# Feed-forward block of a two-layer trunk in fp32 by split products: down product 1 placed between products 3 and 7, gate multiplication later, roundings issued together

## The chip, the cores and the metric

The kernel runs on one core of a Trainium2 chip. Its five engines work side by side: TensorE (PE in the profile) multiplies, VectorE (DVE), ScalarE (ACT) and GpSimd (POOL) work element by element, SyncE (SP) issues transfers; POOL issues some of them too. Each engine takes its instructions in the order in which they were written and waits at the first one whose inputs are not there. The metric is the device time of one execution in microseconds (us), the median of several runs.

## The reference

One sequence of 512 positions, 1024 wide, runs through two layers. Layer 0 mixes with a gated linear recurrence, layer 1 with a stick-breaking attention; behind each mixer stands a feed-forward block of width 2816, and this is what the change is about:

```python
def _swiglu(h, w_gate, w_up, w_down):
    g = h @ w_gate.astype(h.dtype)
    u = h @ w_up.astype(h.dtype)
    return (jax.nn.silu(g) * u) @ w_down.astype(h.dtype)
...
        h = _rmsnorm(x, norm_ffn_g[layer])
        x = x + _swiglu(h, ffn_w_gate[layer], ffn_w_up[layer], ffn_w_down[layer])
```

All inputs and the output are float32.

## The kernel before

**Numbers in two parts.** Every operand of a matrix product is split into a rounded part (high) and what is left (low), and a product is three matmuls: high by high, high by low, low by high. For a weight tile of 128 x 1024 ACT writes the rounded part `wh` (a CAST, line 303), and DVE, or POOL for some tiles, the residual `wl` (a subtraction, line 304). In the profile's names `wh`, `wl` are these; `raw`, `bu`, `bv`, `d`, `dt` are the loaded weights that they come from.

**Seven products for eight.** The two projections up and the projection down are each done by a scheme of the Strassen kind: seven products of half-size blocks take the place of eight, at the price of sums of weights and of results. The products up are called g1 to g7, those down d1 to d7. Sums of weights are partly made by accumulating transfers, issued by POOL (line 92), partly on POOL (`minus`, line 144) and DVE (`sums`, line 164 down, line 116 up). The weights of g3 and g7 lie in `bv`: when g3's tile has been split, a transfer adds onto `bv` what g7 needs.

**Units.** A block of feed-forward goes in six units, u = 0 to 5: units 0 to 4 ("full") take 512 columns each of gate and up, unit 5 (`NU`, the "half unit") 256. From unit 1 on, a unit also does the products down for the columns of the unit before. A full product is two pieces for g (12 matmuls each) and one piece of 12 matmuls for d. `Unit.order` is a list written by hand that sets the program's order; PE, ACT, DVE and POOL keep it exactly. Weights run ahead of the products through one list of pieces: when a piece is used (`chunk`), pieces up to four further are split (`split_one`: ACT's cast and the residual), and up to eleven further are loaded. Split weights have four pairs of buffers, so that a cast also waits until PE is through with the piece four before.

**From one unit to the next.** The step `tt` turns the four results of the unit before, u2 and b5, with PE's transposes into PSUM banks 76, 77 (tb) and 74, 75 (db). `operands1` and `operands2` then make the left operands of the products down from them, first for tb (in `tt`), then for db (steps `o1` and `o2`): copy t, rounded parts `hah`, `hbh`, `hth` on ACT, four reads of the banks into t and the low parts `hal`, `hbl`, `htl` on DVE. d1 reads ha, d2 and d4 hb, the others ht. Where ACT and DVE read the same bank, the later one in the program waits for the earlier one.

**Around the results.** After g6 ACT copies bank A into `u` (line 871), after g3 DVE adds bank B onto it (`u2_add`). After g7 DVE adds bank A onto `b` (b5); g4 goes on accumulating in bank A, so it waits for that addition. After g2 come an addition of r1 and Silu (line 857), after g4 another Silu (line 889). `q1` (line 861) multiplies u2 by the gate of g2, `q2` (line 913) b5 by that of g4. Each down product ends with two additions onto `y` (`dproduct`, line 754); its bank is used again by a later one: d1, d6, d7, d4 share one pair of banks, d2, d5, d3 the other (in the half unit the pairs change places). In the table `mids` stands which of q1, q2 is called between the matmuls of a down product and its additions. Lines 753 and 754 are the helpers for subtractions and additions, 758 the cast of a split, 762 to 764 the three matmuls of a product.

Of the kernel before, what the change touches and what calls it, by code (L numbers as in the profile page):

```python
# [10 lines left out]
F32 = mybir.dt.float32  # L11
# [21 lines left out]
NU = 5  # L33
# [11 lines left out]
class Unit:  # L45
    def __init__(self, kern, l, u):
        self.kern, self.u = kern, u
        self.w = FB if u < NU else FB // 2
        self.np = 2 if u < NU else 1
        self.kt = 2 if u < NU else 4  # L50
        self.src = kern.a["w_gu"][l, 8 * u:8 * u + 4 * self.np]
        self.down = kern.a["w_dn"][l, 4 * (u - 1):4 * u] if u else None
        self.b, self.d = {}, {}
        self.direct = u == NU
        if u == 0:
            self.order = "g1 g5 stats g2 x0 g6 x1 g3 q1 g4 x2 g7 x3"
        elif u < NU:
            self.order = "g5 g1 tt g6 o1 o2 g3 g7 d1 d2 g4 d6 d5 g2 d7 d3 d4"
        else:
            self.order = "g5 g1 tt g6 o1 g3 o2 d1 g2 d2 g7 d6 d5 g4 q2 d7 tn d3 d4"  # L60
        if u == NU - 1:
            self.order = self.order.replace("g2 d7", "g2 q1 d7")
        if u == 1:
            self.order = self.order.replace("g5 g1", "g1 g5")
        self.pieces = []
        for n in self.order.split():
            if n[0] not in "gd":
                continue
            q = int(n[1])
            self.pieces += [Piece(self, q, c) for c in range(self.np)] if n[0] == "g" else [DownPiece(self, q)]  # L70


class Piece:
    LOADS = {1: ("raw", 0), 2: ("raw", 2), 5: ("bu", 0), 3: ("bv", 3)}
    HOME = {1: 1, 2: 2, 5: 5, 6: 5, 4: 5, 3: 3, 7: 3}
    def __init__(self, unit, q, c):
        self.unit, self.q, self.c = unit, q, c
        self.pool = (q, c) == (7, 1) and unit.u > 0 and unit.np == 2
        self.summed = False

    def buf(self, tag, pool, bufs):
# [16 lines left out]
    def load(self):  # L98
        un, kern, q = self.unit, self.unit.kern, self.q
        if q not in self.LOADS:  # L100
            return
        tag, n = self.LOADS[q]
        t = un.b[q, self.c] = kern.raw_buf() if tag == "raw" else self.buf(tag, kern.wp, 2)
        kern.nc.sync.dma_start(t, self.part(n))
        if q == 5:
            self.plus(1)
            kern.chain[self.c] = un
# [25 lines left out]
class DownPiece(Piece):  # L133
# [12 lines left out]
    def load(self):  # L146
        un, kern = self.unit, self.unit.kern
        for k in {1: ("12", "22", "11"), 2: ("21",)}.get(self.q, ()):
            t = un.d[k] = kern.raw_buf() if k in ("11", "21") else self.buf("d" + k, kern.fp, 1)
            kern.nc.sync.dma_start(t, un.down[("11", "21", "12", "22").index(k)])  # L150
        if self.q == 1:
            un.d["t"] = self.buf("dt", kern.fp, 1)
            n = 6 if un.direct else 1
            self.minus("t", "22", "12", n)
            self.minus("12", "12", "11", n + 1)

# [14 lines left out]
class Kern:  # L171
# [554 lines left out]
    def ffn(self, l, gnext):  # L726
        nc, tc = self.nc, self.tc
        mm = nc.tensor.matmul
        E = mybir.EngineType
        with tc.tile_pool(name=f"ffn{l}", bufs=1) as self.fp, \  # L730
# [4 lines left out]
            for i in range(self.used + 1, len(self.chunks)):  # L735
                if isinstance(self.chunks[i], Piece) and not isinstance(self.chunks[i - 1], Piece):
# [3 lines left out]
            db, tb = self.bank[4:6], self.bank[6:]  # L740
            fp = self.fp
            ev = [[fp.tile([P, S], F32, tag=f"{n}{j}", bufs=1, name=f"{n}{j}") for j in range(2)]
                  for n in ("r1", "u2", "b5")]
            r1, u2, b5 = ev
            y = [fp.tile([P, D], F32, tag=f"y{t}", bufs=1, name=f"y{t}") for t in range(NT)]
            ha, hb, ht = ([fp.tile([P, *shape], F32R, tag=f"{n}{i}", bufs=1, name=f"{n}{i}") for i in "hl"]
                          for n, shape in (("ha", (2, HS)), ("hb", (2, S)), ("ht", (2, 4, HS))))
# [5 lines left out]
            sub = lambda o, a, b: nc.vector.tensor_tensor(o, a, b, ALU.subtract)  # L753
            add = lambda o, a, b: nc.vector.tensor_tensor(o, a, b, ALU.add)  # L754

            def split(dst, src):
                h, lw = dst
                nc.scalar.copy(h, src)  # L758
                sub(lw, src, h.bitcast(F32))
# [6 lines left out]
            def turn(fs, banks):  # L766
                for f, b in zip(fs, banks):
                    for t in range(NT):
                        nc.tensor.transpose(b[:, ts(t)], (u2 + b5)[t][:, ts(f)], self.ident)  # L769

            def operands1(p, banks):
                cx = self.tmp()
                nc.scalar.copy(cx, banks[0])
                split([t[:, p] for t in ha], cx[:, T0])
                return cx

            def operands2(p, banks, cx):
                bx, by = banks
                ta, tc_ = (self.tmp() for _ in range(2))
                add(ta[:, T0], cx[:, T1], by[:, T1])  # L780
                sub(tc_[:, T0], cx[:, T0], bx[:, T1])
                sub(ta[:, T1], ta[:, T0], cx[:, T0])
                sub(tc_[:, T1], by[:, T0], ta[:, T1])
                split([t[:, p] for t in hb], by)
                for i, t in enumerate((ta, tc_)):
                    split([o[:, p, 2 * i:2 * i + 2].rearrange("p a b -> p (a b)") for o in ht], t)

# [36 lines left out]
            for u in range(NU + 1):  # L824
                un = self.unit_of()
# [6 lines left out]
                def product(q, out, first=True):  # L832
                    for c in range(un.np):
                        wh, wl = self.chunk()
                        for j in range(2):
                            for i in range(un.kt):
                                k = c * un.kt + i
                                oh, ol = self.ops[k][q]
                                ws = slice(i * w, i * w + w)
                                mm3(out[j][:, :w], oh[:, ts(j)], ol[:, ts(j)], wh[:, ws], wl[:, ws],  # L840
                                    first and k == 0, k == 3)

                def b5_copy():
                    for j in range(2):
                        nc.scalar.copy(b5[j][:, :w], B[j][:, :w])
# [6 lines left out]
                def g2():  # L852
                    product(2, B2)
                    for j in range(2):
                        add(B2[j][:, :w], r1[j][:, :w], B2[j][:, :w])
                    for j in range(2):
                        nc.scalar.activation(B2[j][:, :w], B2[j][:, :w], AF.Silu, scale=rs(j))

                def q1():
                    for j in range(2):  # L860
                        nc.vector.scalar_tensor_tensor(u2[j][:, :w], u2[j][:, :w], nrs(j), B2[j][:, :w],  # L861
                                                       ALU.mult, ALU.mult)
# [59 lines left out]
                def tt():  # L922
                    turn((0, 2), tb)
                    turn((1, 3), db)
                    cx = operands1(0, tb)
                    b5_copy()
                    operands2(0, tb, cx)

                def o1():
                    self.cx = operands1(1, db)  # L930
# [7 lines left out]
                        split([t[:, p] for t in hn], A[p])  # L938

                steps = dict(q1=q1, q2=q2, g1=g1, g2=g2, g3=g3, g4=g4, g5=g5, g6=g6, g7=g7, stats=stats, tt=tt, o1=o1, o2=o2, tn=tn)  # L940
                mids = {6: q2, 7: q1} if u < NU - 1 else {6: q2} if u < NU else {2: q1}
                steps.update({f"d{q}": (lambda q=q: dproduct(q, two, mids.get(q))) for q in range(1, 8)})
                steps.update({f"x{t}": (lambda t=t: None if gnext else turned(t)) for t in range(NT)})
                for n in un.order.split():
# [440 lines left out]
```

## Time and profile before

| what | value |
|---|---|
| median of 3 runs | 1170.92 us (1170.79 to 1173.19) |
| profiled execution, its own time | 1172.12 us |
| its span, first to last instruction | 1170.4 us |
| mean granted clock of TensorE | 0.982 |
| PE, DVE, ACT, POOL busy | 1114.0, 911.0, 711.3, 400.0 us |
| feed-forward blocks in the span | about 167 to 530 and 806 to 1166 us |

Rows of a timeline read: start, duration (us), engine, line, operation, what it writes and from what (buffer numbers left out), shapes, how many in a row, and in brackets how long the engine stood idle before it and what ended that. Full units 1 to 4 of layer 0 have their g7 at 230, 297, 360 and 425 us; the prediction works in unit 3, at 336 to 402 us. In PE's rows the moving operand tells the product: `s` is g7's left operand, `ow` that of g2 to g6, `a` of g1, `hah` d1, `hbh` d2 or d4, `hth` the other down products.

### The profile page before, as it was taken

How to read it: one execution, taken by the hardware profiler on the slowest of the kernel's cores; microseconds unless marked ns; L12 is line 12 of the kernel's file. 1: busy time of each engine (PE TensorE's matmuls, PEld its weight loads, DVE VectorE, ACT ScalarE, POOL GpSimd, SP SyncE). 2: the span in 40 equal slices, each digit the busy share in tenths (PEclk: the TensorE clock that was granted, in tenths of full speed). 3: DMA queues.
4: the chain of work that ended last, by engine and by line, in shares of the span. 5: the costliest groups of instructions: out<-in, count | busy, mean ns of one | idle time of the engine just before them, and what ended most of it. 6: DMA issues, size and time to landing. Idle time of an engine off the chain costs nothing. (4 is left out here: it accounts for less than half of the span.)

```text
span 1170.4 us, 14792 instructions
## 1 busy us (share of the span) xinstructions
PE 1114.0 (95%) x5265; PEld 916.6 (78%) x5265; DVE 911.0 (78%) x1242; ACT 711.3 (61%) x1086; POOL 400.0 (34%) x266
## 2 busy tenths in 40 slices
PE   8999999989998989999999999899989999998987
PEld 6887788778787868878888888778878878787875
DVE  7878886667887868887378898778657797777887
ACT  6698576455545454535479999868654445545454
POOL 2451332344442514115043443412234344342411
PEclk9999999989999989999999999899999999999999
DMA  8422349857575655342243333125966757574421
GB/s 281 153 90 90 109 124 221 177 160 165 129 205 137 182 134 166 91 144 85 76 127 101 100 91 94 52 90 168 217 120 196 158 164 165 137 194 100 143 57 72
DMA packets 48825, 159.87 MB, mean 137 GB/s; under 512 B 6000, under 2 KB 7280, under 8 KB 48752
## 3 DMA queue, kind: packets, MB, share of 16 engines
q1 hardware_dynamic: 36368, 113.84, 28.3%
q0 software_dynamic: 12384, 45.09, 22.1%
q8 instruction: 41, 0.67, 0.2%
q14 instruction: 32, 0.26, 0.1%
HBM read 148.43 MB, written 2.10 MB: 129 GB/s over the span
## 5 line engine op out<-in xcount | busy, mean ns | idle before, releaser
L304 DVE TENSOR_TENSOR wl<-raw,wh 128x1024 fp32r<-128x1024 f32 (+1 forms) x118 | 197.7, 1679 | 59.6 <-ACT wh L303 59.1
L303 ACT CAST wh<-raw 128x1024 fp32r<-128x1024 f32 (+1 forms) x144 | 144.4, 1011 | 96.9 <-PE bank L764 34.6
L762 PE MATMUL bank<-wh,ow 128*128 128x512 f32 (+1 forms) x480 | 179.9, 375 | 2.4 <-DVE u L754 1.8
L764 PE MATMUL bank<-wh,ow 128*128 128x512 f32 (+1 forms) x480 | 178.4, 372 | 0.0
L763 PE MATMUL bank<-wl,ow 128*128 128x512 f32 (+1 forms) x480 | 178.3, 371 | 0.0
L92 POOL DMA_DIRECT2D bu<-w_gu x64 | 56.2, 878 | 223.1 <-DVE wl L304 114.0
L303 ACT CAST wh<-bu 128x1024 fp32r<-128x1024 f32 x66 | 69.4, 1051 | 78.7 <-issue 33.4
L304 DVE TENSOR_TENSOR wl<-bu,wh 128x1024 fp32r<-128x1024 f32 x66 | 82.0, 1249 | 32.2 <-ACT wh L303 31.2
L762 PEld LDWEIGHTS bank<-wh,ow 128*128 128x128 f32 x480 | 90.4, 188 | 19.3 <-DVE u L754 2.6
L349 PE MATMUL bank<-uh,wh 128*128 128x512 f32 x256 | 102.3, 400 | 2.1 <-ACT wh L303 1.4
L764 PEld LDWEIGHTS bank<-wh,ow 128*128 128x128 f32 x480 | 90.4, 188 | 15.7
L763 PEld LDWEIGHTS bank<-wl,ow 128*128 128x128 f32 x480 | 90.5, 188 | 15.4
L351 PE MATMUL bank<-uh,wl 128*128 128x512 f32 x256 | 100.2, 392 | 1.4 <-DVE wl L304 1.4
L350 PE MATMUL bank<-ul,wh 128*128 128x512 f32 x256 | 99.7, 390 | 0.3 <-DVE ul L406 0.3
L304 POOL TENSOR_TENSOR wl<-raw,wh 128x1024 fp32r<-128x1024 f32 (+1 forms) x26 | 59.2, 2278 | 111.9 <-ACT wh L303 111.9
L754 DVE TENSOR_TENSOR y<-y,bank 128x512 f32<-128x512 f32 x140 | 88.9, 678 | 2.4 <-PE bank L764 2.3
L762 PE MATMUL bank<-wh,hth 128*128 128x512 f32 x192 | 75.2, 392 | 4.1 <-DVE y L754 4.1
L763 PE MATMUL bank<-wl,hth 128*128 128x512 f32 x192 | 75.0, 391 | 0.4 <-DVE wl L304 0.4
L764 PE MATMUL bank<-wh,htl 128*128 128x512 f32 x192 | 74.8, 390 | 0.0
L304 DVE TENSOR_TENSOR wl<-bv,wh 128x1024 fp32r<-128x1024 f32 x36 | 49.2, 1366 | 30.8 <-ACT wh L303 29.8
L303 ACT CAST wh<-bv 128x1024 fp32r<-128x1024 f32 x44 | 46.2, 1051 | 40.2 <-DMA bv<-w_gu 29.3
L1135 POOL TENSOR_TENSOR spl<-t,sph 128x512 fp32r<-128x512 f32 (+1 forms) x32 | 36.4, 1159 | 85.7 <-DVE sph L1134 79.8
(258 smaller groups left out, 2844.2 us busy)
## 6 DMA issues: line engine op xcount, KB each, us to landing
bu<-w_gu POOLq DMA_DIRECT2D x64, 512.0 KB, 5.8
raw<-w_gu SPq DMA_DIRECT2D x44, 512.0 KB, 3.5
raw<-w_dn SPq DMA_DIRECT2D x24, 512.0 KB, 5.9
bu<-w_gu SPq DMA_DIRECT2D x22, 512.0 KB, 3.4
bv<-w_gu SPq DMA_DIRECT2D x22, 512.0 KB, 3.5
bv<-w_gu POOLq DMA_DIRECT2D x22, 512.0 KB, 6.3
d<-w_dn SPq DMA_DIRECT2D x20, 512.0 KB, 3.5
raw<-w_qk SPq DMA_DIRECT2D x16, 512.0 KB, 3.4
```

What stands on the lines that cost most here:

```text
L92: kern.soon(lambda: kern.nc.gpsimd.dma_start(t, self.part(n), accum_op=ALU.add))
L303: self.nc.scalar.copy(wh[:, c], raw[:, c])
L304: self.wl_engine(i).tensor_tensor(wl[:, c], raw[:, c], wh[:, c].bitcast(F32), ALU.subtract)
L349: mm(out, lhsT=wh, rhs=xh, start=first, stop=False)
L350: mm(out, lhsT=wh, rhs=xl, start=False, stop=False)
L351: mm(out, lhsT=wl, rhs=xh, start=False, stop=last)
L754: add = lambda o, a, b: nc.vector.tensor_tensor(o, a, b, ALU.add)
L762: mm(out, lhsT=xh, rhs=wh, start=first, stop=False, skip_group_check=True)
L763: mm(out, lhsT=xh, rhs=wl, start=False, stop=False, skip_group_check=True)
L764: mm(out, lhsT=xl, rhs=wh, start=False, stop=last, skip_group_check=True)
L1135: nc.gpsimd.tensor_tensor(sl[:, w], sp[:, w], sh[:, w].bitcast(F32), ALU.subtract)
```

## The change

The diff, complete but for context:

```diff
-            self.order = "g5 g1 tt g6 o1 o2 g3 g7 d1 d2 g4 d6 d5 g2 d7 d3 d4"
+            self.order = "g5 g1 tt g6 o1 o2 g3 d1 g7 d2 g4 d6 d5 g2 d7 d3 d4"
...
-        self.pool = (q, c) == (7, 1) and unit.u > 0 and unit.np == 2
+        self.pool = False
...
-            n = 6 if un.direct else 1
+            n = 6 if un.direct else 3
             self.minus("t", "22", "12", n)
             self.minus("12", "12", "11", n + 1)
...
-            def operands2(p, banks, cx):
+            def operands2(p, banks, cx, mid=None):
                 bx, by = banks
                 ta, tc_ = (self.tmp() for _ in range(2))
+                nc.scalar.copy(hb[0][:, p], by)
+                if mid:
+                    mid()
                 add(ta[:, T0], cx[:, T1], by[:, T1])
                 sub(tc_[:, T0], cx[:, T0], bx[:, T1])
                 sub(ta[:, T1], ta[:, T0], cx[:, T0])
                 sub(tc_[:, T1], by[:, T0], ta[:, T1])
-                split([t[:, p] for t in hb], by)
+                sub(hb[1][:, p], by, hb[0][:, p].bitcast(F32))
...
                     for j in range(2):
                         add(B2[j][:, :w], r1[j][:, :w], B2[j][:, :w])
+                    if u < NU:
+                        silu1()
+
+                def silu1():
                     for j in range(2):
                         nc.scalar.activation(B2[j][:, :w], B2[j][:, :w], AF.Silu, scale=rs(j))

                 def q1():
+                    if u == NU:
+                        silu1()
...
-                    b5_copy()
-                    operands2(0, tb, cx)
+                    operands2(0, tb, cx, b5_copy)
...
-                mids = {6: q2, 7: q1} if u < NU - 1 else {6: q2} if u < NU else {2: q1}
+                mids = {6: q2, 3: q1} if u < NU - 1 else {6: q2} if u < NU else {2: q1}
```

In the full units d1 stands between g3 and g7 instead of behind g7. The second piece of g7 gets its residual on DVE; `pool` of the down pieces is set elsewhere and stays. `hbh` is issued directly behind `hah`, ahead of DVE's four bank reads, and in `tt` ahead of the copies into b5 as well. In units 1 to 3 `q1` moves from d7 to d3; in the half unit Silu of g2 moves into `q1`, behind the splitting that d2 triggers. POOL's two differences of down weights are due two pieces later.

ACT in unit 3 of layer 0, from the cast of g3's second piece on; `bv` are g7's weights, `raw_2709` or `raw_2669` d1's, `raw_2730` d2's. Before:

```order
L303 CAST wh_2833<-bv_2643 128x1024
L303 CAST wh_2850<-bv_2625 128x1024
L871 COPY u_1495<-bank_72 128x512
L871 COPY u_1496<-bank_73 128x512
L773 COPY t_2870<-bank_74 128x512
L758 CAST hah<-t_2870 128x256
L758 CAST hbh<-bank_75 128x512
L758 CAST hth<-t_2874 128x512
L758 CAST hth<-t_2875 128x512
L303 CAST wh_2886<-bv_2643 128x1024
L303 CAST wh_2904<-raw_2709 128x1024
L303 CAST wh_2922<-raw_2730 128x1024
```

The same stretch of ACT now:

```order
L303 CAST wh_2833<-bv_2643 128x1024
L303 CAST wh_2850<-raw_2669 128x1024
L880 COPY u_1495<-bank_72 128x512
L880 COPY u_1496<-bank_73 128x512
L773 COPY t_2870<-bank_74 128x512
L758 CAST hah<-t_2870 128x256
L780 CAST hbh<-bank_75 128x512
L758 CAST hth<-t_2874 128x512
L758 CAST hth<-t_2875 128x512
L303 CAST wh_2886<-bv_2625 128x1024
L303 CAST wh_2904<-bv_2643 128x1024
L303 CAST wh_2922<-raw_2730 128x1024
```

The cast of g7's first piece went from second place to behind the roundings, and d1's cast took its place.

DVE in the same unit, from behind the low parts `htl` on; u are the additions of g3, b those of g7, y those of a down product, and L164 is the sum for d6. Before:

```order
L304 TENSOR_TENSOR wl_2905<-raw_2709,wh_2904 128x1024
L754 TENSOR_TENSOR u_1495<-u_1495,bank_70 128x512
L754 TENSOR_TENSOR u_1496<-u_1496,bank_71 128x512
L304 TENSOR_TENSOR wl_2923<-raw_2730,wh_2922 128x1024
L304 TENSOR_TENSOR wl_2939<-bu_2505,wh_2938 128x1024
L754 TENSOR_TENSOR b_1497<-b_1497,bank_72 128x512
L754 TENSOR_TENSOR b_1498<-b_1498,bank_73 128x512
L304 TENSOR_TENSOR wl_2957<-bu_2527,wh_2956 128x1024
L164 TENSOR_TENSOR raw_2709<-dt_2711,raw_2709 128x1024
L754 TENSOR_TENSOR y_1499<-y_1499,bank_74 128x512
L754 TENSOR_TENSOR y_1500<-y_1500,bank_75 128x512
```

The same stretch of DVE now:

```order
L304 TENSOR_TENSOR wl_2887<-bv_2625,wh_2886 128x1024
L304 TENSOR_TENSOR wl_2905<-bv_2643,wh_2904 128x1024
L754 TENSOR_TENSOR u_1495<-u_1495,bank_70 128x512
L754 TENSOR_TENSOR u_1496<-u_1496,bank_71 128x512
L304 TENSOR_TENSOR wl_2923<-raw_2730,wh_2922 128x1024
L754 TENSOR_TENSOR y_1499<-y_1499,bank_74 128x512
L754 TENSOR_TENSOR y_1500<-y_1500,bank_75 128x512
L304 TENSOR_TENSOR wl_2941<-bu_2505,wh_2940 128x1024
L304 TENSOR_TENSOR wl_2957<-bu_2527,wh_2956 128x1024
L164 TENSOR_TENSOR raw_2669<-dt_2671,raw_2669 128x1024
L754 TENSOR_TENSOR b_1497<-b_1497,bank_72 128x512
L754 TENSOR_TENSOR b_1498<-b_1498,bank_73 128x512
```

The residual of g7's second piece (from `wh_2904`) is new here, and the two additions onto b stand two weight residuals, the sum and two additions onto y further back.

ACT in the half unit of layer 0, from the cast of g7 on; `raw_3498` is d6's sum, `d_265` is d5's weights, `bu_3415` g4's, and the two ACTIVATE rows are Silu of g2. Before:

```order
L303 CAST wh_3806<-bv_3474 128x1024
L303 CAST wh_3827<-raw_3498 128x1024
L857 ACTIVATE bank_70<-bank_70,rsT 128x256
L857 ACTIVATE bank_71<-bank_71,rsT 128x256
L303 CAST wh_3861<-d_265_3494 128x1024
L303 CAST wh_3884<-bu_3415 128x1024
```

The same stretch of ACT in the half unit now:

```order
L303 CAST wh_3806<-bv_3474 128x1024
L303 CAST wh_3827<-raw_3498 128x1024
L303 CAST wh_3859<-d_265_3494 128x1024
L864 ACTIVATE bank_70<-bank_70,rsT 128x256
L864 ACTIVATE bank_71<-bank_71,rsT 128x256
L303 CAST wh_3884<-bu_3415 128x1024
```

Silu went behind the cast for d5.

In units 1 to 3, DVE's two rows of `q1` moved from ahead of the additions of d7 to behind them and behind one more weight residual. POOL's row loses the residual of g7 in every full unit and is otherwise unchanged in order; so is SP's.

## The prediction

> **What bounds the kernel now.** I read the busy shares first, then TensorE's waits, then its granted clock in the stretches that the waits point to, and last the timelines of ACT and DVE there. The busy shares:
>
> ```profile
> PE 1114.0 (95%) x5265; PEld 916.6 (78%) x5265; DVE 911.0 (78%) x1242; ACT 711.3 (61%) x1086; POOL 400.0 (34%) x266
> ```
>
> TensorE (PE) sets the end, so the question is only where it stands still or runs slowly. PE's waits, in total, times and longest:
>
> ```profile
> PE bank L763 <- POOL wl L304: 15.4, 8, 1.9
> PE bank L762 <- ACT wh L303: 10.7, 8, 2.3
> PE bank L762 <- DVE y L754: 5.8, 8, 2.1
> ```
>
> The first two come eight times each: the seventh product of the eight full units (units 1 to 4 of both layers). The table of stretches cuts out that product, from its first matmul to the first one of the next product; the row behind it is a product of the same 24 matmuls, the third product of unit 3, which did not wait. The columns are the stretch and its length, the busy times, the granted clock, and the DMA share:
>
> ```profile
> 230.10:243.26 13.16, 8.69 (x25) 6.13 (x26) 10.77 (x15) 6.74 (x10) 2.36 (x1) 0.74 0.35 105
> 297.30:305.40 8.10, 6.01 (x25) 4.42 (x24) 6.41 (x8) 5.41 (x7) 2.35 (x1) 1.00 0.32 120
> ...
> 1062.63:1073.57 10.94, 7.43 (x25) 5.51 (x24) 9.22 (x13) 5.41 (x7) 2.35 (x1) 0.84 0.15 49
> sum 85.81, PE 59.42 PEld 43.57 DVE 70.48 ACT 45.44 POOL 18.82; mean PE 7.43 PEld 5.45 DVE 8.81 ACT 5.68 POOL 2.35
> 354.50:359.94 5.44, 5.44 (x26) 4.50 (x24) 1.84 (x3) 2.91 (x5) 0.88 (x1) 1.00 0.59 103
> ```
>
> 24 matmuls take 5.44 us when nothing holds them, 0.227 each. Eight times that is 43.5, and the eight took 85.81: **42.3 us are lost in product 7**. The waits make up only 15.4 + 10.7 = 26.1. The rest is in PE's own timeline (start, length, idle before and releaser), unit 3, between the product's two pieces:
>
> ```profile
> 364.15 0.50 PE L762 MATMUL bank<-wh,s 128*128 128x512 f32 x1 [1.33 <-ACT wh L303]
> 366.58 0.80 PE L763 MATMUL bank<-wl,s 128*128 128x512 f32 x1 [1.93 <-POOL wl L304]
> 367.18 0.63 PE L764 MATMUL bank<-wh,s 128*128 128x512 f32 x1
> 367.60 0.63 PE L762 MATMUL bank<-wh,s 128*128 128x512 f32 x1
> ...
> 369.61 0.39 PE L764 MATMUL bank<-wh,s 128*128 128x512 f32 x1
> ```
>
> A matmul's length of 0.39 overlaps the next one's start, so a wait costs its length plus 0.16 (0.39 - 0.227); and behind the two waits the matmuls start 0.42 apart (367.18, 367.60) until the pace is back at 369.61. The granted clock says the same: 0.74 and 0.84 where both waits are long, 1.00 where they add to 2.1 (297.30). The Trainium skill (TensorE: Matmul & The Clock Gate, "What's actually happening") halves the clock after an idle window of about 3.4 us. No single wait here is that long, so by that rule taken wait by wait, product 7 would give back 26.1 + 16 x 0.16 = 28.7 us; the stretches measure 42.3, and I take the measurement.
>
> Why PE waits: ACT and DVE in unit 3.
>
> ```profile
> 356.63 1.05 ACT L303 CAST wh<-bv 128x1024 fp32r<-128x1024 f32 x1 [3.10 <-DMA bv<-w_gu]
> 357.59 1.07 ACT L871 COPY u<-bank 128x512 f32<-128x512 f32 x2
> 361.53 0.59 ACT L758 CAST hbh<-bank 128x512 fp32r<-128x512 f32 x1 [1.95 <-DVE t L753]
> 362.01 1.14 ACT L758 CAST hth<-t 128x512 fp32r<-128x512 f32 x2
> 363.05 1.04 ACT L303 CAST wh<-bv 128x1024 fp32r<-128x1024 f32 x1
> ```
> ```profile
> 361.07 0.43 DVE L753 TENSOR_TENSOR t<-bank,t 128x256 f32<-128x256 f32 x1
> 362.15 0.69 DVE L753 TENSOR_TENSOR hbl<-bank,hbh 128x512 fp32r<-128x512 f32 x1 [0.65 <-ACT hbh L758]
> 362.76 1.28 DVE L753 TENSOR_TENSOR htl<-t,hth 128x512 fp32r<-128x512 f32 x2
> 365.08 2.53 DVE L304 TENSOR_TENSOR wl<-raw,wh 128x1024 fp32r<-128x1024 f32 x1 [1.03 <-ACT wh L303]
> 368.73 1.21 DVE L304 TENSOR_TENSOR wl<-raw,wh 128x1024 fp32r<-128x1024 f32 x1
> 369.86 1.21 DVE L304 TENSOR_TENSOR wl<-bu,wh 128x1024 fp32r<-128x1024 f32 x1
> ```
> ```profile
> 355.14 0.88 POOL L92 DMA_DIRECT2D bv<-w_gu  x1 [6.82 <-DVE wl L304]
> 364.18 2.35 POOL L304 TENSOR_TENSOR wl<-bv,wh 128x1024 fp32r<-128x1024 f32 x1 [8.16 <-ACT wh L303]
> ```
>
> ACT first waits 3.10 for the accumulating load of the first piece of product 7, with the copies of product 6 (u) queued behind it. Then hbh waits 1.95 until DVE has read the same bank four times (last 361.07), DVE's hbl waits 0.65 for hbh, and the cast of the second piece (363.05) stands behind all of it. Its residual on POOL then takes 2.35, while DVE's own residual beside it takes 2.53 against 1.21 to 1.23 elsewhere.
>
> **The change, part by part,** in unit 3; a weight cast costs 1.04 (363.05), a weight residual 1.13 from start to start (368.73, 369.86), a pair of 512-wide adds 1.2 (1.28 for y below, less the overlap), the roundings and bank reads what their rows say.
>
> *Down product 1 between products 3 and 7, roundings together.* ACT now casts down piece 1, loaded long before, at 352.8 where it waited for the load, and copies u when product 6 is through (354.50 in the table, its last bank 354.7), not at 357.59. The first bank-half's chain, changed the same way, hands over about 0.5 earlier. Then t 355.2, hah 355.8, hbh at once 356.1 to 356.7. DVE: hal 356.3, its four bank reads from 356.8 (they now wait for hbh) to 358.3, hbl to 358.9, htl to 360.1. ACT meanwhile hth to 359.0 and the first piece of product 7 to 360.0; DVE's residual of it 360.1 to 361.3. The second piece's load is issued once product 3's second residual is done, so about 354.6 instead of 355.14; with this median (min/median/max, issue to landing)
>
> ```profile
> DMA to landing us min/median/max: 3.4/5.5/10.0
> ```
>
> it is there at 360.1; cast to 361.2, residual, now on DVE, to 362.5. PE, dense: down product 1 at 359.94, product 7 at 362.7, its second piece at 365.4, down product 2 at 368.1, product 4 at 370.8. Down product 1 overwrites the banks that hbl reads last: free at 358.9, margin 1.0. Product 7 has its residuals at 361.3 and 362.5: margins 1.4 and 2.9. Both old waits go. What is late next is DVE, now without a break: u adds to 363.6, residual of down 2 to 364.8, y adds to 366.0, the two residuals of product 4 to 368.3, the sum for down 6 (as wide as a residual) to 369.4, then the b5 additions to 370.6. Product 4 accumulates into the banks they read, bank by bank: first free at 370.0, margin 0.8. Before, two down products covered these additions; now one does. Unit 1 begins late (its loads come later): I allow 0.3 there in each layer. So 42.3 - 0.6 = **41.7 us**. This covers the moved residuals too: 8 x 1.21 more for DVE, of which 2.53 - 1.21 comes back in each unit, because nothing on POOL reads beside it; on the path it costs nothing while the margins of 1.4 and 0.8 hold, else what exceeds them.
>
> POOL's two differences of down pieces keep their place in POOL's row (only their due number changes), SP's row is unchanged, and POOL's next loads no longer stand behind a 2.35 residual: nothing. Down product 7 behind product 4 instead of 1 and 2 before it: no, products 5, 6, 2 and the rest keep their places, nothing.
>
> *Later gate multiplication (L861), units 1 to 3.* Down product 4 adds onto the banks of down product 7 and waits for DVE's y:
>
> ```profile
> 398.17 0.47 PE L762 MATMUL bank<-wh,hbh 128*128 128x512 f32 x1 [0.27 <-DVE y L754]
> 396.03 1.40 DVE L861 SCALAR_TENSOR_TENSOR u<-u,nrs,bank 128x512 f32<-128x512 f32 x2
> 397.34 1.28 DVE L754 TENSOR_TENSOR y<-y,bank 128x512 f32<-128x512 f32 x2
> ```
>
> With the multiplication behind it, y starts at 396.03 and the first bank is free at 396.7, before 397.74 when PE wants it. Six of the eight y waits are these, 0.27 to 0.28 each: 6 x (0.27 + 0.16) = **2.6 us**. The multiplication then stands before the y adds of down product 3; the banks that it reads are next written by product 1 of the next unit, three products later: nothing.
>
> *The half unit (unit 5).* Same order; the roundings and the place of Silu change.
>
> ```profile
> 485.24 0.39 PE L762 MATMUL bank<-wh,ow 128*128 128x256 f32 x1 [0.89 <-DVE u L754]
> 499.32 0.47 PE L762 MATMUL bank<-wh,hth 128*128 128x512 f32 x1 [2.09 <-DVE y L754]
> 478.60 0.59 ACT L758 CAST hbh<-bank 128x512 fp32r<-128x512 f32 x1 [3.39 <-DVE t L753]
> 494.76 0.81 ACT L857 ACTIVATE bank<-bank,rsT 128x256 f32<-128x256 f32 x2 [1.63 <-DVE bank L754]
> 498.50 1.28 DVE L754 TENSOR_TENSOR y<-y,bank 128x512 f32<-128x512 f32 x2
> ```
>
> hbh waits 3.39 for DVE's bank reads; issued at once, the chain hands over 1.0 earlier (0.65 of DVE's wait, and hth no longer stands behind 0.59 of hbh). So down 1 no longer waits for hah, and product 2 starts at 484.25 instead of 485.24. The second chain gives another 0.9. Dense from there, down product 5 would start at 495.4. It needs the y adds, which stood behind the residual of down 5, whose cast stood behind Silu (494.76). With Silu behind that cast, the residual ends at 494.3, the multiplication at 495.1, the first y at 495.7: start 495.8 instead of 499.32, 3.5 us earlier; both layers, **7.0 us**. Lower bound: if the chains give nothing, the order of Silu alone gives about 1.5 each, 3.0.
>
> *Sum.* 41.7 + 2.6 + 7.0 = 51.3. I keep 1.3 back for margins below 1 us that fail in some unit. The profiled execution took 1172.12 (span 1170.4), so 1122.1; the median of the runs shown is 1.2 below it: **1121 us**. Own range of this case: 1115 (no loss left, and small waits such as that for L913 gone too) to 1127 (margins missed by 0.7 in every unit).
>
> **Rivals.**
> 1. *The wait moves to down product 1 or to product 4.* For it: margins of 1.0 and 0.8 after a chain of some twenty steps. Against: every step has its own row. If DVE or ACT is 1.8 us late per unit, PE waits 0.8 to 1.0 more and 0.16, eight times, 8 to 9 us; 3 us late, 18 us: 1130 to 1139.
> 2. *The load of product 7's second piece.* At the slowest landing, 10.0, it is there at 364.6 and its residual at 366.9: PE waits 1.5, and the b5 additions behind it on DVE are late by about as much: 3 x 8 = 24, so 1145 if all units meet it. The median landing and the margin of 2.9 speak against it.
> 3. *DVE becomes the bound.* From down 1 to down 1, unit 2 to unit 3:
>
> ```profile
> 305.40:370.53 65.13, 61.32 (x270) 49.75 (x269) 53.38 (x60) 32.23 (x41) 26.42 (x15) 0.97 0.64 162
> ```
>
> DVE is busy 53.38 of 65.13; shortened by 5 it would be at 89%. If its idle stretches could shrink by only half of 5.3, units would lose 2.6 and not 5.3: half of 41.7 is left out, 1142. Against it: the idle that goes (the 1.03 and 0.65 above among it) lies just where the change works. The Trainium skill (Perfetto Trace Analysis, "Optimizing Scalar/DVE Operations") would, with a saturated DVE, rather move work off it, to GpSimd too, while it doubts that this pair gains; the 2.53 beside POOL's residual agrees with the doubt.
> 4. *Slower.* The sum for down 6 now stands before the b5 additions on DVE, and waits for POOL's difference, which is due two pieces later than before. If POOL were late, DVE, product 4 and PE would stop. It decides from 6.4 us of PE wait per unit (51.3 / 8); the sum would have to start at 375 instead of 368.2. At 8 us per unit: 1121 + 64 = 1185. Against it: POOL's row holds the differences in their old place, which is early:
>
> ```profile
> 338.92 3.27 POOL L144 TENSOR_TENSOR d<-d,raw 128x1024 f32<-128x1024 f32 x1
> ```
>
> This is the second of them; both are done by 342.2, 26 us before the sum.
> 5. *Nothing moves:* ACT stays late for another reason, and the same clock penalty is paid at down 1: 1165 to 1172.
>
> **Chances.** Forecast 0.74; first rival 0.12; second 0.04; third 0.05; slower 0.04; nothing 0.01. 0.2% (2.3 us) is about what a measurement of this kernel tells from no change. Faster 0.95, same 0.01, slower 0.04. The range takes the forecast's own bounds and the first rival up to its middle: 1115 to 1134.
>
> **What would show it.** Right: no POOL residual of bv left; the eight stretches of product 7 near 5.5 us with the clock at 1.00; PE's y waits down from eight to two short ones; down product 5 of the half unit waiting under 0.5; DVE's share of the span up from 78% to about 81%, since its busy time hardly changes. Wrong: PE rows with hah (down 1) waiting for DVE's hbl, ow rows of product 4 waiting for DVE's b, or slow matmuls behind either.

## The result, and the profile after

The changed kernel took 1120.15 us (median of 4 runs, 1118.79 to 1120.95) against 1170.86 for the kernel before on the same chip: ratio 0.956, 95% interval 0.955 to 0.958. The forecast was 1121, in 1115 to 1134. The profiled execution took 1120.95, span 1119.3, 51.1 less than before. The busy shares of the page:

```profile
PE 1095.9 (98%) x5265; PEld 907.9 (81%) x5265; DVE 907.5 (81%) x1250; ACT 711.7 (64%) x1086; POOL 381.9 (34%) x258
```

TensorE's busy time fell by 18 us for the same 5265 matmuls: most of that is pace (matmuls that had started 0.42 apart), a part is the 0.16 of overlap lost at each wait. The other 33 us are idle time. What PE still waits for (total, times, longest):

```profile
PE bank L1120 <- DVE awl L1190: 2.9, 3, 2.3
PE bank L762 <- DVE u L754: 1.7, 2, 0.9
PE bank L762 <- DVE b L922: 1.7, 3, 1.0
...
PE bank L763 <- DVE wl L304: 0.5, 1, 0.5
...
PE bank L762 <- DVE hbl L753: 0.4, 1, 0.4
```

The 15.4 behind POOL, the 10.7 behind ACT's casts and the 5.8 behind y have all gone. The largest entry left lies in the attention block. The stretches of product 7, from its first matmul to the next product's (length, busy times, granted clock, DMA share):

```profile
234.23:239.77 5.54, 5.54 (x25) 4.43 (x24) 5.14 (x7) 4.31 (x6) 0.00 (x0) 1.00 0.58 188
293.86:299.30 5.44, 5.44 (x26) 4.50 (x24) 5.44 (x8) 2.11 (x2) 0.00 (x0) 1.00 0.54 181
...
1023.16:1028.60 5.44, 5.44 (x26) 4.50 (x24) 5.44 (x8) 2.11 (x2) 0.00 (x0) 1.00 0.24 84
sum 43.62, PE 43.62 PEld 35.96 DVE 43.22 ACT 19.10 POOL 0.00; mean PE 5.45 PEld 4.49 DVE 5.40 ACT 2.39 POOL 0.00
```

85.81 became 43.62, which is what 8 x 24 matmuls need. In unit 3, PE at the start of down product 1, of product 7's two pieces and of product 4:

```profile
350.05 0.39 PE L762 MATMUL bank<-wh,hah 128*128 128x512 f32 x1
...
352.77 0.39 PE L762 MATMUL bank<-wh,s 128*128 128x512 f32 x1
...
355.49 0.39 PE L762 MATMUL bank<-wh,s 128*128 128x512 f32 x1
...
360.93 0.39 PE L762 MATMUL bank<-wh,ow 128*128 128x512 f32 x1
```

No row has a bracket, and pieces follow each other after 2.72 = 12 x 0.227. ACT and DVE there:

```profile
345.92 0.41 ACT L758 CAST hah<-t 128x256 fp32r<-128x256 f32 x1
346.23 0.58 ACT L780 CAST hbh<-bank 128x512 fp32r<-128x512 f32 x1
347.97 1.14 ACT L758 CAST hth<-t 128x512 fp32r<-128x512 f32 x2 [1.15 <-DVE t L753]
349.01 2.00 ACT L303 CAST wh<-bv 128x1024 fp32r<-128x1024 f32 x2
```
```profile
348.31 0.68 DVE L753 TENSOR_TENSOR hbl<-bank,hbh 128x512 fp32r<-128x512 f32 x1
...
350.11 2.35 DVE L304 TENSOR_TENSOR wl<-bv,wh 128x1024 fp32r<-128x1024 f32 x2
...
359.31 1.28 DVE L754 TENSOR_TENSOR b<-b,bank 128x512 f32<-128x512 f32 x2
```

In this unit ACT no longer waits for a load: both pieces are cast in one go (349.01), and both residuals run on DVE at their undisturbed 1.2 each. hbh follows hah at once. The half unit:

```profile
461.44 0.39 PE L762 MATMUL bank<-wh,ow 128*128 128x256 f32 x1 [0.88 <-DVE u L754]
472.96 0.47 PE L762 MATMUL bank<-wh,hth 128*128 128x512 f32 x1
```

Down product 5 (472.96) lost its 2.09; product 2 (461.44) kept its 0.88. Down 5 starts 11.52 behind product 2, before 14.08.

### The profile page after: what moved, and what is told of

Same layout as the page of the kernel before. It is cut to its first block, busy times and chain, and to the rows that moved or that the text cites. A ratio compares the mean times of both kernels' runs of the same rounds, so it can differ in the third digit from the quotient of the medians.

```text
span 1119.3 us, 14757 instructions
## 1 busy us (share of the span) xinstructions
PE 1095.9 (98%) x5265; PEld 907.9 (81%) x5265; DVE 907.5 (81%) x1250; ACT 711.7 (64%) x1086; POOL 381.9 (34%) x258
## 4 chain that ended last, share of the span: by engine, by line
PE 68%; DVE 12%; ACT 4%; issue 4%; DMA 3%; POOL 0%; SPq 0%; DVEq 0%; POOLq 0%; ACTq 0%
PE bank L762 14%; PE bank L763 14%; PE bank L764 14%; PE bank L349 6%; PE bank L351 6%; PE bank L350 5%; DVE wl L304 5%; PE bank L1175 3%; DMA bu<-w_gu 2%; ACT wh L303 2%; PE bank L1201 2%; DVE y L754 1%; PE bank L769 1%; PE bank L1120 1%; DMA bv<-w_gu 1%
## 5 line engine op out<-in xcount | busy, mean ns | idle before, releaser
L304 DVE TENSOR_TENSOR wl<-raw,wh 128x1024 fp32r<-128x1024 f32 (+1 forms) x118 | 188.1, 1599 | 44.1 <-ACT wh L303 43.8
L304 DVE TENSOR_TENSOR wl<-bv,wh 128x1024 fp32r<-128x1024 f32 x44 | 58.3, 1336 | 15.3 <-ACT wh L303 15.2
```

The source lines that it names most:

```text
L304: self.wl_engine(i).tensor_tensor(wl[:, c], raw[:, c], wh[:, c].bitcast(F32), ALU.subtract)
```

## The experiments

Twelve kernels ran in three sets, each set on one chip with the kernel before beside it (its medians there: 1172.15, 1175.71, 1175.04). Since chips differ by 0.4%, ratios and profiles are compared. "Lost" is counted from PE's starts: the time from one matmul's start to the next, less the usual distance of its shape; over the whole span 83.8 before, 32.7 after.

### Where the gain comes from: the order, the residual, or the rest

Three kernels take the change apart at product 7. **o1** is the kernel before with the new order alone:

```diff
-            self.order = "g5 g1 tt g6 o1 o2 g3 g7 d1 d2 g4 d6 d5 g2 d7 d3 d4"
+            self.order = "g5 g1 tt g6 o1 o2 g3 d1 g7 d2 g4 d6 d5 g2 d7 d3 d4"
```

> The kernel before with one edit: down product 1 between products 3 and 7 of the full units. POOL's residual, the roundings, the gate multiplication and Silu stay as before. My theory (the order alone gives product 7's second piece the time it lacked): product 7 loses next to nothing, hbh's late rounding costs what it cost in the changed kernel with the roundings apart (about 0.7 per full unit), the y waits (6 x 0.43) and the half unit (7.0) stay: 42 - 6 gained, 1130 to 1137. Rival (the residual on POOL and the late roundings hold product 7 in any order): 1150 or more, with rows of TensorE <- POOL wl L304 above 5 us in total.

**u1** is the opposite: the changed kernel with only this line turned back.

> The changed kernel with down product 1 put back behind product 7; residuals on DVE, roundings together, the later gate multiplication and the later Silu stay. My theory (product 7 lost its time because ACT reached its second piece late, behind the load of the first piece and the roundings): the load of the first piece is again waited for, hbh is rounded about 1.5 us earlier than in the kernel before, so the second piece's cast and its residual (1.21 on DVE, not 2.35 on POOL) still come late: waits of about 0.6 and 1.2 us per full unit, 8 x (0.6 + 1.2 + 2 x 0.16) = 17 us: 1132 to 1140. Rival (the residual on POOL was the cause, the order of the products is indifferent): 1120 to 1122. Rival (all of the gain is the order): within 10 us of the kernel before's 1170.9 less the 7 of the half unit, 1155 to 1165.

**o2** is the kernel before with the residual on DVE alone:

```diff
-        self.pool = (q, c) == (7, 1) and unit.u > 0 and unit.np == 2
+        self.pool = False
```

> The kernel before with one edit: the residual of product 7's second piece on DVE instead of POOL. It takes about 1.2 instead of 2.35, and DVE's own residual beside it loses its slowing (2.53 to 1.2), but DVE does it after that one. My theory: the wait for wl falls from 1.9 to about 0.8 per full unit, the wait for wh (10.7 in all) stays; without the second long wait the matmuls behind it keep their full pace: 8 x (1.1 + about 1.5) = 21 gained, 1145 to 1157. Rival (the residual on POOL was all of the cause): 1130 or less. Rival (indifferent, as in the changed order): 1169 to 1173.

The sums of the eight stretches of product 7, for o1, u1 and o2 in this order:

```profile
sum 44.04, PE 44.04 PEld 35.89 DVE 44.04 ACT 20.47 POOL 15.56; mean PE 5.50 PEld 4.49 DVE 5.50 ACT 2.56 POOL 1.95
```
```profile
sum 56.13, PE 47.56 PEld 35.50 DVE 54.92 ACT 41.51 POOL 0.00; mean PE 5.95 PEld 4.44 DVE 6.87 ACT 5.19 POOL 0.00
```
```profile
sum 69.54, PE 54.16 PEld 39.27 DVE 61.98 ACT 45.67 POOL 0.00; mean PE 6.77 PEld 4.91 DVE 7.75 ACT 5.71 POOL 0.00
```

| kernel | median us | ratio to before, interval | span | lost in product 7 |
|---|---|---|---|---|
| before | 1170.86 | 1 | 1170.4 | 42.3 |
| o2: residual on DVE | 1160.82 | 0.989 (0.986 to 0.992) | 1157.5 | 26.0 |
| u1: all but the order | 1140.44 | 0.972 (0.968 to 0.976) | 1137.6 | 12.6 |
| o1: the order alone | 1140.31 | 0.970 (0.968 to 0.972) | 1137.3 | 0.5 |
| changed | 1120.15 | 0.956 (0.955 to 0.958) | 1119.3 | 0.1 |

The order alone clears product 7, with POOL's 2.46 still in its stretches. The rest of the change alone clears 30 of the 42, so the two gains overlap and must not be added. With the old order kept, taking the residual off POOL clears 16 (o2), and the remaining parts of the change, the earlier rounding among them, another 13 (u1 against o2); the last 13 need the new order, which by itself clears all of it. What o1 lacks is outside: y still costs it

```profile
PE bank L762 <- DVE y L754: 5.8, 8, 2.1
```

the second gate multiplication makes product 2 wait six times (2.9 in all, before 0.6), and the half unit waits as before. Its gain is 35.4 on its chip, where I expected 34 to 41 from 1171. In u1 the load is waited for again (first row), and one wait of the old pair is left (second row):

```profile
352.16 1.05 ACT L303 CAST wh<-bv 128x1024 fp32r<-128x1024 f32 x1 [2.38 <-DMA bv<-w_gu]
```
```profile
360.16 0.50 PE L763 MATMUL bank<-wl,s 128*128 128x512 f32 x1 [0.76 <-DVE wl L304]
```

I had expected 0.6 and 1.2 there; in unit 3 the first wait was gone and the second 0.76. u1's time still came in at the upper end because unit 1, whose loads come late, lost 2.2 and 3.5 in its stretches (7.62 and 8.95), and it pays the wait for b (L922) in seven units, 2.3 in all. In o2 TensorE's wait for ACT's casts stays, at 9.0 after 10.7, as foretold; its gain of 13 to 15 is a little less than the 14 to 26 expected, since three of its stretches kept the slow pace (below).

### POOL's residual in the new order

**u2** puts the residual of the second piece back on POOL in the changed kernel (the line of o2 turned back).

> The changed kernel with the residual of product 7's second piece back on POOL (2.35 us there, DVE's own beside it 2.53 instead of 1.21). My theory: in the changed order that piece is cast at about 351.3 in unit 3 of the profile after, POOL would be done by 354 and DVE's residual beside it at most 1.3 us later than now, while TensorE needs the piece at 355.5; DVE gives away 1.21 and gets 1.32 of slowing: within 1 us of the changed kernel, 1119 to 1122. Rival (POOL's residual was the cause of the waits L763 <- wl L304, 15.4 us in the kernel before): 8 x (1.9 + 0.16) = 16 us: 1136.

1118.35, ratio 0.954 (0.950 to 0.958): the same as without it. In unit 3:

```profile
351.02 2.49 POOL L304 TENSOR_TENSOR wl<-bv,wh 128x1024 fp32r<-128x1024 f32 x1 [5.77 <-ACT wh L303]
```
```profile
352.36 2.23 DVE L304 TENSOR_TENSOR wl<-raw,wh 128x1024 fp32r<-128x1024 f32 x1
```

POOL is done at 353.5, about 2 us ahead of PE. DVE gives 1.2 away and is slowed by 1.0 beside it (2.23 for 1.22). So the 15.4 us that the list of waits put down to POOL's residual before were mostly lateness that POOL handed on: the cast ahead of it came late. Mostly, because in the old order a faster residual did help (o2, 16 of the 42); in the new one the 2.4 on POOL fit into the time that there is.

### The roundings and Silu

**u3** rounds hbh behind the bank reads again:

```diff
-                nc.scalar.copy(hb[0][:, p], by)
                 if mid:
...
-                sub(hb[1][:, p], by, hb[0][:, p].bitcast(F32))
+                split([t[:, p] for t in hb], by)
```

> The changed kernel with hbh rounded behind DVE's four bank reads again (the second chain's b5 copy stays ahead of them). My theory: DVE's chain hands over 0.65 (its wait for hbh) to 0.9 us later; the margins of about 1.0 ahead of down product 1 and product 4 in the profile after are nearly used up: 0 to 0.5 per full unit and 1 to 2 per half unit, together 4 to 8: 1124 to 1128. Rival (the margins are larger than the rows say, DVE catches up): 1120 to 1122. Rival (ACT's wait for DVE's bank reads, 1.95 us per unit in the kernel before, was the main cause of product 7's loss): 8 x 2 = 16: 1136.

1130.23, ratio 0.963 (0.959 to 0.967); span 10.1 longer than the changed kernel's. ACT's wait of 1.95 is back to the digit:

```profile
351.09 0.59 ACT L758 CAST hbh<-bank 128x512 fp32r<-128x512 f32 x1 [1.95 <-DVE t L753]
```

Yet product 4 loses only 0.2 to 0.3 in six full units and 0.75 in one: its margin nearly held. As much went to a place that I had not costed, the second gate multiplication, for which product 2 waits:

```profile
PE bank L762 <- DVE b L921: 3.3, 5, 1.1
```

The half units lose 3.4 and 3.3 where the changed kernel loses 1.4: 1.9 each, inside the 1 to 2 expected. In the full units it is 6.3 together, more than the 0 to 4: 2.2 at product 4, 2.4 more than now at product 2, and 1.8 more in unit 1 ahead of product 4. So the roundings are worth about 10 us here, six of it in full units, and that only roughly: c0 below, the changed kernel once more, lost 2.8 less in the feed-forward blocks than the profile after. The rival's 16, in product 7, did not come: ACT's full wait is back and product 7 loses next to nothing. In the new order that wait is harmless to product 7; what it cost there in the old order, u3 can't tell, and no run has it alone.

**u5** issues Silu of the half unit at once, as before.

> The changed kernel with the half unit's Silu issued at once behind product 2's adds, as in the kernel before. My theory: down product 5 of the half unit again waits for DVE's y, by the 1.6 us that ACT waits for those adds (L857 in the kernel before): 1.5 per layer, 3 us: 1122 to 1124.5, with a row of TensorE <- y L754 of 1.3 to 1.8 us in each layer. Rival (the earlier chain alone took that wait away): 1120, no such row.

1126.01, ratio 0.959 (0.955 to 0.964), which on the first chip's 1170.9 would be 1123. Down product 5 waits again, in both layers:

```profile
476.52 0.47 PE L762 MATMUL bank<-wh,hth 128*128 128x512 f32 x1 [1.63 <-DVE y L754]
```

Its loss of 1.87 and 1.88 against 0.27 and 0.25 gives 3.2 us for the order of Silu. The times alone would not show it, since the intervals of u5 and of the changed kernel overlap. With u3's 1.9 in each of the two half units for the roundings, that makes 7.0, all that the half units gained.

### The margin of product 4, and the price of a wait

**d7** and **d10** make DVE late by a known dose ahead of the b5 additions, with results used nowhere:

```diff
+                    for _ in range(7 if 0 < u < NU else 0):
+                        sub(self.tmp(), u2[0], u2[1])
                     for j in range(2):
                         add(b5[j][:, :w], b5[j][:, :w], A[j][:, :w])
```

> The changed kernel with seven extra subtractions of 128x512 on DVE, about 0.6 us each by the residuals of twice the width, ahead of the b5 additions of each full unit (their result is used nowhere). DVE gives product 4 its banks 4.2 us later; with a margin of 1.0 TensorE waits once for about 3.2 us in each of eight units. My theory of the sum: 8 x (3.2 + 0.16) = 27 without a change of clock: 1147. If a wait of this length already slows the matmuls behind it (the kernel before lost 1.7 us per unit to a slower pace behind two waits that added to 2.8 to 3.3 us): 1147 + 8 x 1.7 = 1161. The Trainium skill (TensorE: Matmul & The Clock Gate, "What's actually happening") has the clock halve only after an idle window of about 3.4 us: by that, 1147. Rival (DVE catches up because the margins are far larger than 1.0): under 1135. Rival (DVE is the bound, so each us of work on it costs one): 8 x 4.2 = 34: 1154.

> The same with ten extra subtractions: DVE 6 us later, TensorE waits once for about 5 us in each full unit. Without a change of clock 8 x (5 + 0.16) = 41: 1161. With a slower pace behind the wait, of the size that the kernel before showed in its worst units (1.7 to 3 us): 1175 to 1185, and the granted clock of the stretch below 0.9. Rival (DVE as the bound, all of it paid): 8 x 6 = 48: 1168 with the clock at 1.00.

d7 took 1160.21 (0.987, 0.985 to 0.989; span 40.4 above the changed kernel's), d10 1180.53 (1.0045, 1.003 to 1.006; span 57.3 above). The dose in d7, and what PE made of it in two units:

```profile
371.32 4.30 DVE L753 TENSOR_TENSOR t<-u,u 128x512 f32<-128x512 f32 x7
375.53 1.29 DVE L754 TENSOR_TENSOR b<-b,bank 128x512 f32<-128x512 f32 x2
```
```profile
313.91 0.47 PE L762 MATMUL bank<-wh,ow 128*128 128x512 f32 x1 [3.26 <-DVE b L754]
...
376.37 0.47 PE L762 MATMUL bank<-wh,ow 128*128 128x512 f32 x1 [3.26 <-DVE b L754]
...
377.71 0.63 PE L764 MATMUL bank<-wh,ow 128*128 128x512 f32 x1
378.13 0.63 PE L762 MATMUL bank<-wh,ow 128*128 128x512 f32 x1
...
380.69 0.48 PE L762 MATMUL bank<-wh,ow 128*128 128x512 f32 x1
```

The seven subtractions put the b5 additions back by 375.53 - 371.32 = 4.21. PE waits 3.26 and so starts 3.26 + 0.16 = 3.42 late: 0.79 of the dose cost nothing, and that is the margin, forecast 0.8. In d10 they put them back by 6.01, 1.80 more, and PE waits 5.08, 1.82 more: past the margin each us on DVE costs one.

The same wait of 3.26 is followed by the full pace in unit 2 and by starts 0.42 apart in unit 3. The stretches of product 4 behind it, unit 3 first:

```profile
376.37:381.81 5.44, 5.44 (x17) 4.32 (x18) 4.77 (x4) 0.83 (x1) 5.36 (x3) 0.69 0.84 163
313.91:319.35 5.44, 5.44 (x24) 4.50 (x25) 5.44 (x5) 1.72 (x2) 5.36 (x2) 1.00 0.86 161
```

Six units of d7 waited this long; three of them lost 3.50 in all, three 5.07 to 6.15. The other two waited 3.99 and 3.81 and both fell to the slow pace. In d10 all eight lost 1.4 to 2.9 on top of waits of 5.06 to 6.22. So neither of my two prices was right by itself: the slow pace came in three of six units at 3.26 and in every one at 3.8 and more, and what decides at equal waits no run here shows. The Trainium skill (TensorE: Matmul & The Clock Gate, "What's actually happening") says that the activity is judged in windows of about 3.4 us that run freely. The first part of that would fit equal waits with unequal ends, and a slow stretch in unit 3 from about 377.4 to 380.7, 3.3 long; the longest of the three, in layer 1, lasted 5.5. That an idle window is needed does not fit: in o2 two waits of 1.08 and 0.76 with one matmul between them were followed by the slow pace, and so was one wait of 2.10 in a half unit of o1 (the second view below).

```profile
365.34 0.50 PE L762 MATMUL bank<-wh,s 128*128 128x512 f32 x1 [1.08 <-ACT wh L303]
366.60 0.50 PE L763 MATMUL bank<-wl,s 128*128 128x512 f32 x1 [0.76 <-DVE wl L304]
...
367.43 0.63 PE L763 MATMUL bank<-wl,s 128*128 128x512 f32 x1
367.85 0.63 PE L764 MATMUL bank<-wh,s 128*128 128x512 f32 x1
```
```profile
1101.54 0.47 PE L762 MATMUL bank<-wh,hth 128*128 128x512 f32 x1 [2.10 <-DVE y L754]
...
1103.72 0.63 PE L762 MATMUL bank<-wh,hth 128*128 128x512 f32 x1
1104.15 0.63 PE L763 MATMUL bank<-wl,hth 128*128 128x512 f32 x1
```

### Two more waits, and the differences' due time

**c0** is the changed kernel again, on the chip of the next three.

> The changed kernel as it is, timed again on the chip of the next three, so that differences of a few us are taken on one chip: ratio to the kernel before 0.955 to 0.958.

1120.77, ratio 0.954 (0.952 to 0.956). The profiled execution lost nothing in unit 1 of layer 0 ahead of product 7 or at down product 1, where the profile after lost 2.2; at product 2 it lost 1.8 in four units.

**u6** gives POOL's differences their earlier due number back (`n = 6 if un.direct else 1`).

> The changed kernel with POOL's two differences of down pieces due as early as in the kernel before. My theory (they keep their place in POOL's row and are done long before the sum that reads them): no change, within 0.2% of the changed kernel. Rival (their due time helped): 2 us or more slower.

1121.88, ratio 0.955 (0.953 to 0.958): not to be told from c0. In POOL's row a load now went between the two differences, and unit 1 waited for b5 twice (1.2 in all), so a gain of the new due time of a us or so is not excluded.

**b1** moves two steps on DVE:

```diff
-            self.order = "g5 g1 tt g6 o1 o2 g3 d1 g7 d2 g4 d6 d5 g2 d7 d3 d4"
+            self.order = "g5 g1 tt g6 o1 o2 g3 d1 g7 d2 g4 q2 d6 d5 g2 d7 d3 d4"
...
-                mids = {6: q2, 3: q1} if u < NU - 1 else {6: q2} if u < NU else {2: q1}
+                mids = {3: q1} if u < NU - 1 else {} if u < NU else {2: q1}
...
-                        wh, wl = self.chunk()
+                        wh, wl = self.chunk(3 if u == NU and q == 3 else None)
```

> The changed kernel with two steps earlier on DVE: the second gate multiplication (L922) right behind product 4 and not in down product 6, ahead of the residual of product 2's second piece, and in the half unit the u additions ahead of the residual of down product 2. They aim at the largest waits left of TensorE in the units, L762 <- b L922 (1.7 us in three) and L762 <- u L754 (1.7 in two), each with 0.16 to 0.25 beside it. My theory: DVE was idle ahead of both, so both waits go and nothing else comes: 3 to 4.5 us less than the changed kernel, 1116 to 1117. Rival (the residuals that now come later are waited for instead): within 1 us of the changed kernel, with new rows of L763 <- wl L304.

**b3** adds POOL's residual to it.

> The same two steps, and the residual of product 7's second piece on POOL as in the kernel before, which took the time of the changed kernel within 0.2% when it was tried alone. My theory: 0 to 2 us less than without it, since DVE has 1.2 us less per unit ahead of the b5 additions: 1115 to 1117. Rival (POOL and DVE slow each other and a margin near 1 us fails): 2 to 8 us more, 1118 to 1125.

b1 took 1116.80 (0.951, 0.948 to 0.953), b3 1117.84 (0.952, 0.949 to 0.954). The first step worked: no wait for b (L922) at product 2 is left. The second did not, and its rival came true; the wait for u became one for the residual that had been put behind it:

```profile
463.86 0.50 PE L763 MATMUL bank<-wl,hbh 128*128 128x512 f32 x1 [0.76 <-DVE wl L304]
```

1.02 to 1.04 lost there instead of 1.1 to 1.3 in each layer. With 0.5 less at the transposes that end the two half units, the places where the edits work give 2.7. The span fell by 3.4: unit 1 of layer 0 took about 2 of the 2.7 back, and 2.5 came from outside the feed-forward blocks. So the time falls on the forecast partly by luck: one of the two steps did not work. The intervals of the ratios overlap, but all five runs of b1 (1115.69 to 1118.80) lie below all five of c0 (1119.45 to 1121.54), by 4.0 us in the medians; 2.7 is what the trace can put down to the edits. POOL's residual adds nothing to it.

## Why the prediction was right, point by point

- **Product 7, 42.3 lost, 41.7 back.** Measured 42.2 in the stretches. The steps came true to within 0.2: down product 1 at 350.05 is 9.89 earlier than forecast, since earlier units were faster too; moved by that, hah was forecast for 345.91 (345.92), hbl's end for 349.01 (348.99), the second residual's end for 352.6 (352.46), the first b5 bank free at 360.1 (359.95). In unit 3 the second piece was cast with no wait for its load. That the order is enough is shown by o1, that POOL's residual does no harm in it by u2. In the old order the residual had its part in the loss (o2).
- **The unit 1 allowance, 0.3 per layer,** was too small in layer 0 of this execution, where 0.74 and 0.39 were lost to residuals ahead of product 7 and 1.1 at down product 1, against 0.5 lost ahead of the stretch before: 1.7 net. In c0 the same places lost nothing, so this size changes from one execution to the next.
- **y waits, 2.6.** All six gone. Each was worth 0.51 start to start (six rows of 0.51 to 0.52), so 3.1: besides the 0.27 and the 0.16 that I added, the matmul behind each wait started 0.08 late.
- **Half unit, 7.0.** 4.89 and 4.88 lost before, 1.42 and 1.38 after: 7.0. Down 5 starts 11.52 behind product 2, forecast 11.55. The wait of product 2 for u, on which I had said nothing, stayed at 0.88; what went there was hah's. u5 gives 3.2 to Silu (forecast at least 3.0).
- **1.3 kept back for margins.** The margin at product 4 held in every unit (0.79 by d7), that at down product 1 in all but unit 1 of layer 0. What failed was one I had not listed: product 2 waiting for the second gate multiplication, 2.4 lost in three units where before two lost 1.1. That this is 1.3 more, just what I had kept back for other places, is luck. DVE's residuals ahead of it run beside POOL's work and take 2.6 to 2.7 instead of 1.2, here in unit 3; that this makes it late was not tried by itself:

```profile
368.23 2.72 DVE L304 TENSOR_TENSOR wl<-raw,wh 128x1024 fp32r<-128x1024 f32 x1 [0.62 <-ACT wh L303]
```

- **The sum.** 42.2 + 3.1 + 7.0 - 1.7 - 1.3 = 49.3 of the span's 51.1. Another 1.5 came from outside the feed-forward blocks, which the change does not touch (0.4 ahead of the first, 1.1 between the two), and 0.3 I can't place; without the 1.5 I would have been 0.7 too low rather than 0.9 too high. The mechanism and its large terms were right, but that the sum is right to 1 us is luck: too much in some terms and too little in others cancelled.
- **Rivals.** The moved wait (1) does appear in the changed kernel, once: down product 1 of unit 1 of layer 0 waits for DVE, the sign that I had named for being wrong, and loses 1.1 there and not 8 to 18.

```profile
232.07 0.50 PE L762 MATMUL bank<-wh,hah 128*128 128x512 f32 x1 [0.36 <-DVE hbl L753]
```

Waits for hbl or b5 of 0.2 to 1.3 stand in most of the other changed kernels too, and in the doses by intent. The late load (2): in unit 1 of each layer the cast of the second piece waits 0.57 for its load, and product 7 loses 0.1 in one of them and nothing in the other. DVE as the bound (3): from down 1 to down 1 the same stretch became

```profile
291.14:350.05 58.91, 58.91 (x269) 49.01 (x268) 48.65 (x60) 32.44 (x43) 23.25 (x14) 1.00 0.71 179
```

58.91 for 65.13, all of it PE's own work. DVE is busy 48.65 of it, 83% and not the 89% that I had worked out with its 53.38 left as they were: in this stretch its idle time fell by 1.5 only and its busy time by 4.7. Over four units the idle time did shrink as the argument needs. From unit 1's `hal` of the second bank-half to that of unit 5's first, in layer 0, before and after:

```profile
231.49:476.70 245.21, 230.44 (x1039) 189.06 (x1038) 191.82 (x214) 124.71 (x161) 97.68 (x56) 0.97 0.62 159
229.32:453.85 224.53, 223.65 (x1047) 186.20 (x1046) 189.53 (x217) 125.24 (x162) 88.08 (x52) 1.00 0.69 176
```

DVE idles 35.0 where it idled 53.4, which is 18.4 of the 20.7 gained. L164 waiting for POOL (4) happened nowhere: in unit 3 it runs 358.18 to 359.4, right behind the residuals.
- **What would show it** all did: no POOL residual of bv, clock 1.00 in the eight stretches, y waits not even two, 0.27 lost at down 5, DVE at 81%. Of the signs of being wrong, the wait for hbl came in one unit of eight.

## What to carry to other kernels

When an engine waits for the last link of a chain of in-order queues, the list of waits names the link and not what made it late: go back along the queues to the first instruction that stood waiting, here a cast waiting for a load, and give it other work ahead that is ready. Two repairs of the same lateness overlap (in product 7, 30 us by all but the order and 42 by the order alone, 42 together), so each is priced by undoing it in the full version, not by adding; and what undoing costs holds for that version only. A margin can be measured by a dose: put work whose result nobody uses ahead of the instruction, and the dose less the delay of the start that it causes is the margin.

## What the runs showed of the hardware that I had not expected

Equal waits do not cost the same: 3.26 us of TensorE's waiting was followed by 3.3 to 5.5 us at about half pace (starts 0.42 instead of 0.227 apart) in three of six units and by none in the other three. One wait of 2.10 sufficed in a half unit of o1, and 1.84 in two waits in a full unit of o2, while 3.8 or more brought it in all ten units of the two doses that waited so long. Breaking up a pause with one matmul did not protect the pace in o2.
